# ConvFFN's two projections by Strassen's scheme, in two stages with the gated product in DRAM scratch

## The chip, the cores and the metric

The kernel runs on one core of a Trainium2 chip. The metric is device time in microseconds (us) of one execution; lower is better. The core's engines work side by side and wait for each other through semaphores: PE multiplies matrices into PSUM, DVE and POOL do elementwise work, ACT does elementwise functions, SP issues DMAs. DVE and ACT read PSUM; POOL works on SBUF alone.

## The reference, cut to what matters

One layer of a diffusion backbone with 1024 latent tokens of width 1024 and a 256-token context. The change concerns its last part:

```python
D_MODEL, SEQ, GRID_W, D_FF = 1024, 1024, 64, 2816

def conv_ffn(h, rows, w_up, conv_w, conv_b, w_down):
    b, n, _ = h.shape
    u = (h @ w_up).reshape(b, rows, n // rows, 2 * D_FF)      # 1024 -> 5632
    u = dwconv2d(u, conv_w, conv_b).reshape(b, n, 2 * D_FF)   # 3x3 depthwise, 16 x 64 grid
    gate, val = jnp.split(u, 2, axis=-1)
    return (jax.nn.gelu(gate) * val) @ w_down                 # 2816 -> 1024

...
x = x + g1 * merge_mixers(...)                                # ends in the output projection
x = x + g2 * conv_ffn(modulate(x, norm2_g, sh2, sc2), rows, ffn_w_up, ffn_conv_w, ffn_conv_b, ffn_w_down)
return rms_norm(x, final_g)
```

All of it is float32.

## The kernel before, in words

**Products.** Each float32 operand is split into two parts of type fp32r, hi + lo (`Weight.split`, `copy`, `sub`: ACT rounds to hi, DVE or POOL subtracts to get lo), and each block product is three matmuls, hi*hi + hi*lo + lo*hi (`mm3`). A matmul takes a 128x128 block of weights and 512 columns.

**Up-projection.** The 5632 channels are 44 tiles of 128: 22 pairs n of a gate tile and a value tile. A unit (`ffn_mm`) is one tile for all 1024 tokens: 8 blocks of the input width x 2 halves of the tokens x 3 = 48 matmuls into a PSUM tile `big` of two banks (three such tiles, and two of one bank, `sm`). Norm2's output stands transposed in SBUF (`H2`, written by `turn`), as hi and lo.

**Convolution.** `conv` starts each tile on ACT (the middle tap, with the bias), then eight taps follow on DVE, each one instruction that reads the unit in PSUM and adds to an accumulator in SBUF (L1391). `glu` applies gelu on ACT and multiplies gate by value on POOL (L1398; the last on DVE); the product is split into hi and lo and stays in SBUF (`G`).

**Down-projection.** For each two pairs, `down` multiplies 8 token tiles x 2 halves of the width x 2 blocks x 3 = 96 matmuls, and DVE adds each result to the residual `x[t]` in SBUF (L1475). `w_rows` multiplies the weights by the gate g2 on POOL (L97). So up- and down-products alternate, and a pair's taps lie between the down-products' adds. `down_last` takes the final norm along.

**Order.** Instructions are issued in the order of the code; each engine works through its own in order. SBUF is a set of slots of 4 KB per partition (`Slots`), handed out first in, first out. Weights are loaded and split ahead of use (`ahead`).

## Time and profile before

| | |
|---|---|
| time, median of 3 runs | 1547.22 us (1543.91 to 1547.32) |
| profiled execution, first to last instruction (its span) | 1541.3 us |
| what lies around the span: median less span | 5.9 us |
| PE busy | 1465.7 us, 95% |
| DVE busy | 1085.6 us, 70% |
| ACT busy | 523.7 us, 34% |
| POOL busy | 529.0 us, 34% |
| DMA | 109.30 MB, 71 GB/s over the span |

The profiled execution has no time of its own beside its span; the 5.9 us are taken for it. A busy share is an average over stages, so each stage has to be read by itself. ConvFFN's first convolution starts at 803 us, so the stage that changes is nearly half of the span.

### The profile page before, as it was taken

The page shows a single profiled execution, that of the slowest core. Times are in us where ns is not written, and L with a number is a line of the kernel's source. Part 1 is how long each engine was busy: PE and PEld are TensorE (multiplying, and loading weights), DVE is VectorE, ACT ScalarE, POOL GpSimd, SP SyncE. Part 2 cuts the span into 40 slices and gives each one's busy share as a digit, 9 for nine tenths or more (in the row PEclk, how much of TensorE's full clock was granted, in tenths as well). Part 3 has the DMA queues.
Part 4 walks back from the last instruction along what each step waited for, and adds up shares of the span by engine and source line. Part 5 has one row for each costly group of instructions (what it writes and reads, how often), then busy time and mean ns, then how long its engine had stood idle before and what let it go on. Part 6 is the DMA issues. An engine that isn't in the chain of part 4 may idle for free.

```text
span 1541.3 us, 16621 instructions
## 1 busy us (share of the span) xinstructions
PE 1465.7 (95%) x6725; PEld 1187.5 (77%) x6725; DVE 1085.6 (70%) x1193; ACT 523.7 (34%) x616; POOL 529.0 (34%) x269
## 2 busy tenths in 40 slices
PE   5999999998999689979999999999999999999994
PEld 4788888877888578868878787887878888887873
DVE  5768677856125986496668786868668686776887
ACT  6566777663110123242243130312222121222224
POOL 2211221122001553283053454425444342533343
PEclk9999999999999899999999999999999999999997
DMA  9211111101115344513030210112011111211102
GB/s 380 92 34 35 35 35 42 41 28 55 41 41 187 129 130 144 187 41 110 28 123 14 69 55 28 55 42 68 28 55 55 36 46 42 69 42 41 41 1 110
DMA packets 35069, 109.30 MB, mean 71 GB/s; under 512 B 3813, under 2 KB 8224, under 8 KB 34992
## 3 DMA queue, kind: packets, MB, share of 16 engines
q1 hardware_dynamic: 33552, 105.88, 20.2%
q10 hardware_dynamic: 1184, 2.11, 0.5%
q8 instruction: 53, 0.87, 0.2%
q0 software_dynamic: 256, 0.25, 0.1%
q14 instruction: 24, 0.20, 0.0%
HBM read 104.02 MB, written 4.19 MB: 70 GB/s over the span
## 4 chain that ended last, share of the span: by engine, by line
PE 53%; DVE 5%; ACT 1%; issue 1%; DVEq 0%; ACTq 0%
PE big L192 38%; PE sm L192 14%; DVE s L1234 1%; DVE t L453 1%; DVE s L136 1%; ACT s L1505 0%; PE sm L1318 0%; DVE s L336 0%; PE big L1221 0%; DVE s L1233 0%; DVE s L1232 0%; DVE s L1235 0%; DVE h2f L1323 0%; DVE s L1509 0%; DVE s L1311 0%
## 5 line engine op out<-in xcount | busy, mean ns | idle before, releaser
L192 PE MATMUL big<-s,s 128*128 128x512 f32 (+1 forms) x4548 | 1071.0, 395 | 9.8 <-DVE s L136 7.1
L192 PEld LDWEIGHTS big<-s,s 128*128 128x128 f32 (+1 forms) x4548 | 849.3, 188 | 211.2 <-DVE s L136 8.8
L1391 DVE SCALAR_TENSOR_TENSOR s<-big,rest,s 128x945 f32<-128x945 f32 (+2 forms) x352 | 429.2, 1220 | 120.4 <-issue 74.3
L136 POOL TENSOR_TENSOR s<-s,s 128x1024 fp32r<-128x1024 f32 (+1 forms) x132 | 316.9, 2418 | 294.4 <-ACT s L129 143.7
L129 ACT ACTIVATE s<-s 128x1024 fp32r<-128x1024 f32 (+4 forms) x170 | 167.5, 1022 | 261.9 <-DVE mid L921 62.1
L192 PE MATMUL sm<-s,s 128*128 128x512 f32 (+1 forms) x1176 | 253.4, 375 | 0.0
L192 PEld LDWEIGHTS sm<-s,s 128*128 128x128 f32 x1176 | 204.3, 188 | 47.6 <-DVE s L1475 6.2
L1378 ACT ACTIVATE s<-big,rest 128x1024 f32<-128x1024 f32 x44 | 53.1, 1207 | 428.2 <-PE big L192 428.2
L1398 POOL TENSOR_TENSOR s<-s,s 128x1024 f32<-128x1024 f32 x21 | 50.4, 2401 | 313.4 <-DVE s L1391 313.4
L1475 DVE TENSOR_TENSOR s<-sm,s 128x512 f32<-128x512 f32 x160 | 109.9, 687 | 53.7 <-PE sm L192 53.7
L136 DVE TENSOR_TENSOR s<-s,s 128x1024 fp32r<-128x1024 f32 (+3 forms) x62 | 92.0, 1492 | 65.3 <-ACT s L129 51.7
L791 POOL TENSOR_TENSOR s<-s,s 128x1280 f32<-128x1280 f32 x8 | 25.3, 3156 | 190.9 <-ACT s L787 190.9
L908 POOL TENSOR_TENSOR s<-s,s 128x1024 f32<-128x1024 f32 x8 | 21.1, 2644 | 127.4 <-PE big L192 120.7
L754 DVE SCALAR_TENSOR_TENSOR s<-big,par,s 128x1023 f32<-128x1023 f32 (+1 forms) x24 | 30.8, 1282 | 34.2 <-ACT s L751 33.6
L97 POOL TENSOR_TENSOR s<-s,s 128x1024 f32<-128x1024 f32 x22 | 53.1, 2412 | 0.0
L894 DVE TENSOR_TENSOR s<-big,s 128x1024 f32<-128x1024 f32 x8 | 9.8, 1224 | 61.1 <-PE big L192 61.1
L336 DVE SCALAR_TENSOR_TENSOR s<-s,s,s 128x1024 f32<-128x1024 f32 x28 | 43.5, 1555 | 1.0 <-DMA s<-in_mod_w_dram 0.5
L786 ACT ACTIVATE s<-big,rest 128x1024 f32<-128x1024 f32 x32 | 35.8, 1117 | 24.7 <-PE big L192 17.8
L816 DVE SCALAR_TENSOR_TENSOR s<-s,s 128x1280 f32<-128x1280 f32 x16 | 23.7, 1479 | 16.2 <-ACT s L812 16.2
L192 PE MATMUL big<-s,ghi 128*128 128x512 f32 x128 | 34.9, 394 | 0.0
L1221 PE MATMUL big<-s,s 126*128 126x512 f32 (+2 forms) x104 | 26.6, 353 | 8.3 <-DVE s L1233 8.3
L637 ACT ACTIVATE s<-big 128x1024 f32<-128x1024 f32 x8 | 8.1, 1022 | 67.6 <-PE big L192 60.8
(187 smaller groups left out, 1013.3 us busy)
## 6 DMA issues: line engine op xcount, KB each, us to landing
s<-in_mod_w_dram SPq DMA_DIRECT2D x48, 512.0 KB, 4.8
s<-in_ffn_w_up_b_dram SPq DMA_DIRECT2D x44, 512.0 KB, 3.5
s<-in_w_in_b_dram SPq DMA_DIRECT2D x32, 512.0 KB, 4.5
s<-in_ffn_w_down_dram SPq DMA_DIRECT2D x22, 512.0 KB, 3.4
s<-in_x_dram SPq DMA_DIRECT2D x16, 512.0 KB, 5.8
s<-in_w_lru_out_b_dram SPq DMA_DIRECT2D x8, 512.0 KB, 3.4
s<-in_w_o_dram SPq DMA_DIRECT2D x8, 512.0 KB, 5.8
out_dram<-s SPq DMA_DIRECT2D x5, 512.0 KB
```

The source lines that it names most:

```text
L97: self.k.nc.gpsimd.tensor_tensor(self.raw, self.raw, self.scale(), op=OP.mult)
L129: self.nc.scalar.activation(out, in_, AF.Copy)
L136: (self.nc.vector if eng == "dve" else self.nc.gpsimd).tensor_tensor(out, a, b, op=OP.subtract)
L192: return [lambda x=x: nc.tensor.matmul(x[0], x[1], x[2], start=x[3], stop=x[4]) for x in calls]
L336: nc.vector.scalar_tensor_tensor(self.acc, t, col, self.acc, op0=OP.mult, op1=OP.add)
L754: nc.vector.scalar_tensor_tensor(u[:, lo:hi], z[:, lo + s:hi + s], tap[t], u[:, lo:hi], op0=OP.mult, op1=OP.add)
L786: nc.scalar.activation(lat, ps, AF.Sigmoid, bias=col)
L1221: nc.tensor.matmul(x, w, y, start=id(x) not in seen, stop=id(x) not in [id(c[0]) for c in calls[i + 1:]])
L1378: nc.scalar.activation(acc, ps, AF.Identity, bias=self.par["fcb"][:, ti:ti + 1], scale=self.fcw(4, ti))
L1391: nc.vector.scalar_tensor_tensor(o, i, w, o, op0=OP.mult, op1=OP.add))
L1398: (nc.gpsimd if eng == "pool" else nc.vector).tensor_tensor(g, g, v, op=OP.mult)
L1475: nc.vector.tensor_tensor(x, ps, x, op=OP.add)
```

## The change

Strassen's scheme replaces the 8 block products of a 2x2 by 2x2 block product by 7, with sums of blocks ahead of and behind them.

- **Up.** The 2x2 blocks are: gate and value tile of pair n; halves of the input width; halves of the tokens. `turn0` and `turn1` form the token side once (B11, T1, T2, T3, B21, B22, T4, as hi and lo). Per pair, POOL forms the weights' sums (`up_sums`, and one in `up_split`), POOL makes all their lo parts, and `up_product` does 7 products of 4 x 3 = 12 matmuls of 512 columns. Partial sums are kept in PSUM; ACT copies four banks, DVE adds two (`up_join`). Each pair takes two of four PSUM tiles that fill PSUM.
- **The product goes to DRAM** (`G[n]`, stored by `glu`); the residual goes there too (`x1`) and is read again later. All of the up-stage comes before the down-stage.
- **Down.** Seven products one after the other, in the order 1, 2, 6, 7, 5, 4, 3 (`DOWN`), each a sum over 11 steps i (two blocks of `G`); a step is 4 x 3 = 12 matmuls. For each step `down_load` brings blocks of `G` (or the sums S2, S3 stored in DRAM scratch), `down_prep` forms sums on DVE and splits both operands: hi by ACT, lo of `fa` by POOL, lo of `fb` by DVE. `evacuate` combines the results of a product during the next one, with g2 applied by POOL, and does the final norm.

The core of the diff (names of the unchanged helpers as before):

```diff
+        def turn1(kp, pss):
...
+            v.tensor_tensor(f11, f12, f11, op=OP.subtract)
+            split("T1", kp, f11, "dve")
+            v.tensor_tensor(t2, f22, f11, op=OP.subtract)
+            split("T2", kp, t2, "dve")
+            v.tensor_tensor(f12, f22, f12, op=OP.subtract)
+            v.tensor_tensor(f21, f21, t2, op=OP.subtract)
+            split("T3", kp, f12, "pool")
+            split("B22", kp, f22, "pool")
+            split("T4", kp, f21, "dve")
...
+    PRODUCTS = (("A11", "B11", "a0"), ("S1", "T1", "v1"), ("S2", "T2", "a1"), ("A12", "B21", "a0"),
+                ("S3", "T3", "v0"), ("S4", "B22", "a1"), ("A22", "T4", "v0"))
...
+    def up_join(self, n):
+
+        nc, u = self.nc, self.U[n]
+        for b, x in (("a1", "p5"), ("v1", "u3")):
+            o = self.bank(n, b)
+            nc.vector.tensor_tensor(o, o, u[x], op=OP.add)
...
+                if n:
+                    if i == 1:
+                        self.taps(n - 1, "gt", 8)
...
+                    if i == 4:
+                        self.taps(n - 1, "vt", 5)
+            self.up_join(n)
+            if n:
+                self.taps(n - 1, "vt", 8)
+                self.gelu(n - 1)
+        self.down()
...
+    def down_ahead(self, s, loads=4, preps=2):
...
+        elif p == 2:
+
+            y = st[0]
+            v.tensor_tensor(x[:, 1], y[:, 0], y[:, 1], op=OP.subtract)
+            nc.sync.dma_start(self.S3[i], x[:, 1])
+            v.tensor_tensor(we[:, L], we[:, R], we[:, L], op=OP.subtract)
+            fb = wo[:, L]
+        elif p == 6:
+
+            v.tensor_tensor(fa, fa, x[:, 1], op=OP.subtract)
+            nc.sync.dma_start(self.S2[i], fa)
+            fb = x[:, 1]
+            v.tensor_tensor(fb, wo[:, R], we[:, L], op=OP.subtract)
...
+        for f, eng in ((fa, "pool"), (fb, "dve")):
+            t = sl.get([128, 2, 512], F32R, any_=True)
+            self.copy("act", t[:, 0], f)
+            self.sub(eng, t[:, 1], f, t[:, 0].bitcast(F32))
...
+        def add(t, d, bank, other):
+
+            e = H[d]
+            r = temp()
+            v.tensor_tensor(r, bank, other, op=OP.add)
+            nc.gpsimd.tensor_tensor(r, r, self.g2row[:, e], op=OP.mult)
+            v.tensor_tensor(y[t][:, e], y[t][:, e], r, op=OP.add)
+            square(t, d)
...
+                elif p == 4:
+                    add(4 + j, 0, b, at(w, j))
+
+                    r = temp()
+                    nc.gpsimd.tensor_tensor(r, at(u, j), self.g2row[:, H[1]], op=OP.mult)
+                    nc.gpsimd.tensor_tensor(y[j][:, H[1]], y[j][:, H[1]], r, op=OP.add)
...
+                self.down_ahead(s, *((4, 2) if p != 3 else (6, 5)))
...
+                mm(s, bank, range(4), i == 0, i == 10)
+                sl.free(*self.ready.pop(s))
+                s += 1
+                if i == 1 and before:
+                    evacuate(*before)
```

In the last product (p = 3) the last four steps are done together, token tile by token tile, so that `evacuate` of the first tile can start before the last is done.

The change moves instructions on each engine. Three places follow; names are tiles (`s_...` an SBUF slot, `ug` and `uv` a pair's PSUM tiles, `dn` a PSUM tile of the down-stage, `r` a temporary, `big` and `sm` the PSUM tiles of before).

DVE in the middle of ConvFFN, before: the taps of a pair (L1391) between the adds of the down-products (L1475).

```order
L1475 TENSOR_TENSOR s_5490<-sm,s_5490 128x512 x2
L1391 SCALAR_TENSOR_TENSOR s_8130<-big,rest,s_8130 128x15x63
L1391 SCALAR_TENSOR_TENSOR s_8394<-big,rest,s_8394 128x15x63
L1391 SCALAR_TENSOR_TENSOR s_8394<-big,rest,s_8394 128x960
L1391 SCALAR_TENSOR_TENSOR s_8394<-big,rest,s_8394 128x15x63
```

DVE at the end of a pair n of the up-stage now (L1532 is a tap, L1512 a join; `s_8262` is the value accumulator of pair n - 1, `s_8407` the gate accumulator of pair n):

```order
L1532 SCALAR_TENSOR_TENSOR s_8262<-uv,rest,s_8262 128x16x63 x2
L1512 TENSOR_TENSOR ug<-ug,p_8302 128x512
L1512 TENSOR_TENSOR uv<-uv,u_8361 128x512
L1532 SCALAR_TENSOR_TENSOR s_8262<-uv,rest,s_8262 128x15x63
L1532 SCALAR_TENSOR_TENSOR s_8262<-uv,rest,s_8262 128x960
L1532 SCALAR_TENSOR_TENSOR s_8262<-uv,rest,s_8262 128x15x63
L1532 SCALAR_TENSOR_TENSOR s_8407<-ug,rest,s_8407 128x15x63
```

The adds of the down-products have left this stretch; DVE goes from 16 taps of one pair through two joins to 16 taps of the next.

DVE in the seven forms of the tokens now, first of four blocks (L1353 to L1358 are the sums of `turn1`, L138 the lo parts; nothing of it stood before the change):

```order
L1353 TENSOR_TENSOR s_5317<-s_5668,s_5317 128x512
L138 TENSOR_TENSOR s_5650<-s_5317,s_5648 128x512
L1355 TENSOR_TENSOR t_5679<-s_5668,s_5317 128x512
L138 TENSOR_TENSOR s_5654<-t_5679,s_5652 128x512
L1357 TENSOR_TENSOR s_5668<-s_5668 128x512
L1358 TENSOR_TENSOR s_5317<-s_5317,t_5679 128x512
L138 TENSOR_TENSOR s_5666<-s_5317,s_5664 128x512
```

These seven come four times before the first pair's products can be finished.

DVE in the down-stage now, product 6, where the results of product 2 are taken (L1675 and L1678 form a step's sums, L138 is lo of `fb`, L1741 and L1743 are the two halves of `add`):

```order
L1675 TENSOR_TENSOR s_9553<-s_9553 128x512
L1678 TENSOR_TENSOR s_9553<-s_9254,s_8907 128x512
L138 TENSOR_TENSOR s_9600<-s_9553,s_9600 128x512
L1741 TENSOR_TENSOR r<-dn,s_9331 128x512
L1743 TENSOR_TENSOR s_9618<-s_9618,r 128x512
L1741 TENSOR_TENSOR r<-dn,s_9331 128x512
L1743 TENSOR_TENSOR s_9620<-s_9620,r 128x512
```

and POOL at the same place (L138 is lo of `fa`, L1742 the factor g2 of `add`):

```order
L138 TENSOR_TENSOR s_9547<-s_9505,s_9547 128x512
L138 TENSOR_TENSOR s_9573<-s_9529,s_9573 128x512
L138 TENSOR_TENSOR s_9597<-s_9553,s_9597 128x512
L1742 TENSOR_TENSOR r<-r,s_4445 128x512 x4
L138 TENSOR_TENSOR s_9653<-s_9579,s_9653 128x512
```

Before the change POOL had no part in adding results to the residual, and DVE made no sums of operands.

## Rows read from the trace of the kernel before

**Rows 1.** The page's first line.

```profile
span 1541.3 us, 16621 instructions
```

**Rows 2.** Windows: a stretch in the middle of ConvFFN, busy time by engine, clock, DMA.

```profile
core 0: us, PE busy (x) PEld busy (x) DVE busy (x) ACT busy (x) POOL busy (x), PEclk, DMA share, GB/s
1000.00:1200.00 200.00, 200.00 (x864) 160.96 (x863) 146.01 (x145) 43.59 (x42) 85.98 (x36) 1.00 0.15 48
```

**Rows 3.** Timeline, 1000 to 1070: start, length, engine, line, what, count, idle before.

```profile
1008.55 44.62 PE L192 MATMUL big<-s,s 128*128 128x512 f32 x192
...
1021.16 10.03 DVE L1391 SCALAR_TENSOR_TENSOR s<-big,rest,s 128x945 f32<-128x945 f32 x8 [10.61 <-issue]
...
1053.01 17.37 PE L192 MATMUL sm<-s,s 128*128 128x512 f32 x74
```

**Rows 4.** DVE reading PSUM: taps (ns min/median/max), adds (mean), and two in a row.

```profile
L1391 DVE SCALAR_TENSOR_TENSOR s<-big,rest,s x352: 1191/1206/1271, 804.1 to 1498.8; 128x945 f32<-128x945 f32 x88, 128x1008 f32<-128x1008 f32 x44, 128x960 f32<-128x960 f32 x44
...
L1475 DVE TENSOR_TENSOR s<-sm,s 128x512 f32<-128x512 f32 x160 | 109.9, 687 | 53.7 <-PE sm L192 53.7
...
1000.35 0.69 DVE L1475 TENSOR_TENSOR s<-sm,s 128x512 f32<-128x512 f32 x1 [0.31 <-PE sm L192]
1000.96 1.26 DVE L1391 SCALAR_TENSOR_TENSOR s<-big,rest,s 128x1008 f32<-128x1008 f32 x1
```

**Rows 5.** Timeline: DVE operations on SBUF beside POOL's, and one alone (748.81).

```profile
660.76 29.51 POOL L136 TENSOR_TENSOR s<-s,s 128x512 fp32r<-128x512 f32 x13 [3.09 <-ACT s L129]
...
663.19 2.20 DVE L1235 TENSOR_TENSOR s<-s,s 128x1024 f32<-128x1024 f32 x1
...
672.02 2.32 DVE L136 TENSOR_TENSOR s<-s,s 128x1024 fp32r<-128x1024 f32 x1
...
748.81 0.69 DVE L136 TENSOR_TENSOR s<-h2f,s 128x512 fp32r<-128x512 f32 x1
...
1510.03 2.40 POOL L1506 TENSOR_TENSOR s<-s,s 128x1024 f32<-128x1024 f32 x1 [26.99 <-ACT s L1505]
...
1510.42 2.03 DVE L453 TENSOR_TENSOR t<-r 128x1 f32<-128x1 f32 x1
```

**Rows 6.** Groups by form: an ACT copy, the convolution's start, a POOL subtraction (mean ns).

```profile
L129 ACT ACTIVATE s<-s 128x512 fp32r<-128x512 f32 x16 | 9.2, 624 | 27.7 <-DVE s L1235 23.6 <-issue 4.1
...
L1378 ACT ACTIVATE s<-big,rest 128x1024 f32<-128x1024 f32 x44 | 53.1, 1207 | 428.2 <-PE big L192 428.2
...
L136 POOL TENSOR_TENSOR s<-h2f,s 128x512 fp32r<-128x512 f32 x4 | 5.2, 1289 | 8.2 <-DVE h2f L1323 8.2
```

**Rows 7.** Timeline, from the output projection to ConvFFN's first convolution.

```profile
787.87 0.33 PE L1318 MATMUL sm<-ident,s 128*128 128x128 f32 x1 [1.61 <-DVE s L1311]
...
788.24 0.78 ACT L1322 ACTIVATE s<-sm,cols,a 128x512 fp32r<-128x512 f32 x1 [3.42 <-PE sm L1318]
...
802.89 1.21 ACT L1378 ACTIVATE s<-big,rest 128x1024 f32<-128x1024 f32 x1 [1.94 <-PE big L192]
```

**Rows 8.** Windows as in Rows 2: heavy loads at the start, and a wait of PE.

```profile
10.00:20.00 10.00, 6.62 (x36) 6.04 (x37) 5.64 (x18) 8.20 (x15) 0.00 (x0) 1.00 1.03 406
20.00:30.00 10.00, 6.93 (x61) 4.90 (x59) 7.86 (x14) 6.33 (x11) 3.27 (x2) 1.00 1.03 420
...
550.00:555.00 5.00, 2.72 (x14) 2.05 (x13) 3.28 (x5) 1.60 (x3) 2.57 (x2) 0.94 0.32 98
555.00:560.00 5.00, 5.00 (x30) 4.80 (x30) 4.90 (x9) 0.00 (x0) 0.76 (x2) 0.72 0.63 189
```

**Rows 9.** Timeline, the end: square sums, their root, the last scaling.

```profile
1531.28 0.58 ACT L1525 ACTIVATE sm<-s 128x512 f32<-128x512 f32 x1
1531.80 0.19 ACT L1525 ACTIVATION_READ_ACCUMULATOR sm<-s 128x1 f32 x1
1532.57 0.15 DVE L1536 TENSOR_TENSOR ss<-ss,half 128x1 f32<-128x1 f32 x1
...
1534.15 3.08 DVE L1509 SCALAR_TENSOR_TENSOR s<-s,r,s 128x512 f32<-128x512 f32 x3
```

More of the change, by code (lines that the diff above doesn't have):

```diff
@@ L1313, in turn, with rest, form @@
-        def turn(c, k):
-            if k % 2 == 0:
-                H2[c, k // 2] = [sl.get([128, 2, 512], F32R, any_=True) for _ in range(2)]
-            ps = self.sm()
+            def rest():
+                nc.vector.tensor_scalar(n, x[t], r(), None, op0=OP.mult)
+                nc.sync.dma_start(self.x1[t], x[t])
+                sl.free(x[t])
+            return rest
+        self.B = {}
+        f0 = {}
+        def form(name):
+            self.B[name] = [[sl.get([128, 2, 512], F32R, any_=True) for _ in range(2)] for _ in range(2)]
@@ L1352, in out_proj @@
                     ws[i // 6].done()
-                    if i < 24:
-                        self.ahead(4, 2, 2)
+                    if i // 6 < len(early):
+                        early[i // 6]()
             if t == 7:
@@ new lines, in out_proj @@
+        for n in range(2):
+            self.up_banks(n)
+        for n, bank in ((0, "a1"), (0, "v0"), (1, "a1")):
+            self.up_touch(n, bank)
+        for i in (0, 3):
+            self.up_product(0, i)
+        vt = self.U[1]["v"]
+        pss = [vt[:, 0:512], vt[:, 512:]]
+        for kp in range(4):
+            turn1(kp, pss)
+            if kp in (0, 2):
+                self.up_product(1, 0 if kp == 0 else 3)
+        self.up_touch(1, "v0")
+    PRODUCTS = (("A11", "B11", "a0"), ("S1", "T1", "v1"), ("S2", "T2", "a1"), ("A12", "B21", "a0"),
+                ("S3", "T3", "v0"), ("S4", "B22", "a1"), ("A22", "T4", "v0"))
@@ new lines, in up_banks, with bank, up_touch, up_product @@
+    def up_banks(self, n):
+        u = self.U[n]
+        u["g"], u["v"] = [self.pp.tile([128, 1024], F32, name=x, tag="up", bufs=4) for x in ("ug", "uv")]
+    def bank(self, n, b):
+        t = self.U[n]["g" if b[0] == "a" else "v"]
+        return t[:, 512:] if b[1] == "1" else t[:, 0:512]
+    def up_touch(self, n, b):
+        x = self.B["B11"][0][0][:, 0, :]
+        self.nc.tensor.matmul(self.bank(n, b), x[:, 0:128], x, start=True, stop=True)
+    def up_product(self, n, i):
+        nc, u = self.nc, self.U[n]
+        name, form, b = self.PRODUCTS[i]
+        w, (bh, bl) = u["w"].pop(name), self.B[form]
+        o = self.bank(n, b)
+        fresh = i in (0, 1)
+        for k in range(4):
+            hi, lo = [w[:, j, k * 128:(k + 1) * 128] for j in range(2)]
+            h, l = [x[k // 2][:, k % 2, :] for x in (bh, bl)]
+            for m, (x, y) in enumerate(((hi, h), (hi, l), (lo, h))):
+                first = fresh and k == 0 and m == 0
+                nc.tensor.matmul(o, x, y, start=first, stop=k == 3 and m == 2, skip_group_check=not fresh)
+        self.sl.free(w)
+        if i == 0:
+            self.copy("act", self.bank(n, "a1"), o)
+        elif i == 1:
+            u["p5"] = self.gp.tile([128, 512], F32, name="p5", tag=("ghi", "graw")[n % 2])
+            self.copy("act", u["p5"], o)
+        elif i == 2:
+            self.copy("act", self.bank(n, "v0"), o)
+        elif i == 4:
+            u["u3"] = self.gp.tile([128, 512], F32, name="u3", tag=("glo", "rb")[n % 2])
+            self.copy("act", u["u3"], o)
@@ new lines, in gelu, with glu, taps @@
+    def gelu(self, n):
+        g = self.U[n]["ga"]
+        self.nc.scalar.activation(g, g, AF.Gelu_apprx_tanh)
+    def glu(self, n):
+        nc, u = self.nc, self.U[n]
+        nc.gpsimd.tensor_tensor(u["ga"], u["ga"], u["va"], op=OP.mult)
+        self.sl.free(u["va"])
+        nc.sync.dma_start(self.G[n], u["ga"])
+        self.sl.free(u["ga"])
+        del self.U[n]
+    def taps(self, n, x, count):
+        t = self.U[n][x]
+        for _ in range(min(count, len(t))):
+            t.popleft()()
@@ new lines, with down_plan @@
+    DOWN = (1, 2, 6, 7, 5, 4, 3)
+    def down_plan(self):
+        self.st = {}
+        self.wd = {}
+        self.S2 = [self.dp.tile([128, 512], F32, name=f"S2_{i}") for i in range(11)]
+        self.S3 = [self.dp.tile([128, 512], F32, name=f"S3_{i}") for i in range(11)]
+        self.dl = self.dq = 0
+        self.steps = [(p, i) for p in self.DOWN for i in range(11)]
+        self.ready = {}
+    def down_ahead(self, s, loads=4, preps=2):
+        n = len(self.steps)
+        while True:
+            if self.dq < self.dl and self.dq < min(n, s + preps + 1) and self.sl.room_all() >= 2:
+                self.down_prep(self.dq)
+                self.dq += 1
+            elif self.dl < min(n, s + loads + 1) and self.sl.room_all() >= 5:
+                self.down_load(self.dl)
+                self.dl += 1
+            else:
+                break
```

502 lines of the change are left out of this document (291 added, 211 removed).

## The prediction

> **What bounds the kernel now.** I read first the windows over ConvFFN: in 200 us PE is busy for all 200, DVE for 146, POOL for 86, ACT for 44, at a granted clock of 1.00 (the upper level, 2.4 GHz) [rows 2]. So matmuls set the time of this stage. Their price comes from the timeline: 192 matmuls take the time from 1008.55 to 1053.01, 0.2316 us each [rows 3]. ConvFFN has 2112 matmuls up and 1056 down; at this price 734 us of the span of 1541.3 [rows 1]. The second thing to see is DVE: 146 of 200 us is little slack. Its taps cost 10.03 us for eight, 1.254 us each [rows 3], and hardly vary (1.19 to 1.27 us) whatever POOL does [rows 4].
>
> The third is how DVE and POOL go together. In the merge before the output projection POOL needs 29.51 us for 13 subtractions of 512 columns, 2.27 us each [rows 5], where one alone takes 1.29 [rows 6]; DVE's operations of 1024 columns on two SBUF tiles take 2.2 to 2.3 us beside it, and one of 512 alone 0.69 (so about 1.25 for 1024). Thirteen times 1.28 plus ten times 1.25 is 29.2: the two engines take turns, an operation at a time. The end shows it as clearly: a DVE operation on a single column, L453, lasts 2.03 us, until POOL's of 1510.03 ends at 1512.43 [rows 5]. The taps and the adds read one tile in PSUM and one in SBUF and are not held up [rows 4]. So for this kernel: **DVE operations with both inputs in SBUF, and POOL's, add up; those with an input in PSUM don't.**
>
> **The change, part by part.**
>
> *Matmuls.* Up 22 x 7 x 12 = 1848 (and four to open banks), down 7 x 11 x 12 = 924: 396 fewer, 91.7 us if PE stays the bound. A pair up is 84 matmuls, 19.45 us; a step down is 12, 2.78 us.
>
> *Up to the first pair.* The norm of the last tokens ends at 787.87, as before [rows 7]. Then `turn1` forms its operands for four blocks. DVE can begin at 790.0: 8 transposes and two ACT operations of 0.78 us [rows 7] lie ahead. I take 0.62 us for a DVE operation of 512 columns behind another (the next starts 0.61 later [rows 4]), 0.69 where another engine waits for it, 0.62 for an ACT copy and 1.28 for POOL's [rows 6], and 0.05 for each hand-over. A block: sum, ACT copy, lo part, 0.69 + 0.05 + 0.62 + 0.05 + 0.62 = 2.03 us, for T1 and again for T2; then a sum (0.62), and POOL's subtraction waits for the ACT copy until 0.67 behind it; POOL, DVE's last lo part and POOL again take turns, 0.67 + 1.28 + 0.62 + 1.28 = 3.85. Together 8.5 us; four blocks 34, to 824.0. PE has 48 matmuls of this time and mostly waits. POOL then has two lo parts of the first pair's weights (826.6), and PE the products S3 and S4: the first needs those lo parts from 825.3 on and ends at 827.6, the second at 830.4. Before, the first convolution began at 802.9 [rows 7]; now DVE's join (0.69) and ACT's start (1.21 [rows 6]) put the first tap at 832.4. **So 28 us are lost here**, nothing hides them, since no other products are there.
>
> *The pairs.* DVE has 16 taps and two joins a pair, 16 x 1.254 + 2 x 0.62 = 21.3 us; PE has 19.45. Before, the down-products' matmuls lay beside the taps; now none do. The next pair needs the PSUM tiles of the last but one, so PE can lead no further: its second product waits for the last three taps. From there it needs five products, 13.9 us, until the join can run, and DVE has 13 taps, 16.3 us, in front of it; so DVE never waits, and is the bound. 336 taps and 42 joins: 421.3 + 26.0 = 447.3 us. **The up-stage ends at 1279.7**, 1.9 us a pair above PE's. POOL has 11 operations of 512 and one of 1024 a pair, some 16.5 us, beside taps that it doesn't hold up; ACT about 11.
>
> *The down-stage, from DVE and POOL.* PE's part is 77 x 2.78 = 214 us, 30.6 a product. A step costs:
> - Products 2, 6, 5, 3: `fa` is a sum, so the chain is DVE's sum 0.69, ACT 0.62, POOL's lo 1.28 and DVE's lo behind it 0.62, with hand-overs 3.3 us. A second sum of DVE fits into ACT's time.
> - Product 4: two sums, 0.62 + 0.69, POOL 1.28, lo 0.62: 3.2. Product 7: one sum, 2.6, so PE's 2.78. Product 1 has no sums.
>
> Steps are prepared two ahead, so a delay of some 3 us is covered, not one that repeats. What DVE needs, counted from 1279.7:
> - Product 1: the last pair's 16 taps (20.1) and eight lo parts with about 0.3 of waiting each (7.4): 27.5.
> - Product 2: a step loads 1.31 MB and stores 0.26 MB. DMA reached 406 to 420 GB/s at most [rows 8]; at 410 that is 3.84 us a step. Two steps are loaded early: 2 x 3.3 + 9 x 3.84 = 41.2, to 68.7.
> - Product 6: 36.4, and `evacuate` of product 2: four times DVE's add, POOL's g2, DVE's add, 0.69 + 1.28 + 0.69 + 0.1 = 2.75, during which DVE's queue stands: 11.0. To 116.1.
> - Product 7: 31.1, its four adds from PSUM within; to 147.2. Product 5: 36.4 + 2.5 = 38.9, to 186.1.
> - Product 4: 35.2 + 4 x 3.33 (one more add) = 48.5, to 234.6.
> - Product 3: 36.4, and between its steps `evacuate` of product 4, four times three POOL operations and a DVE one, 4 x 4.46 = 17.8, and the norm of four token tiles, 1.7 + 4 x 1.25 = 6.7; to 295.5. The loads of its last three steps stand on SP behind the stores of these tiles, so they cannot come earlier.
> - The end: 12 matmuls (2.8), then four token tiles one after the other on DVE and ACT, each 0.69 + 0.69 + 0.58 + 0.19 for the sum of squares, 1.58 to the root (1532.57 to 1534.15 [rows 9]), 1.25 for scaling and 0.3 of hand-overs, 5.3: 21.2; and the last store, 4.1 as now (from 1537.23 to the span's end [rows 1, 9]). To 323.6.
>
> **Sum:** 1279.7 + 323.6 = 1603.3 us of span, 62 above 1541.3. The median lies 5.9 above the span, so 1609 us, 4.0% slower. The 92 us saved on PE are spent where PE waits: 28 at the entry, 41 in the pairs (21.3 against 19.45, 22 times), the rest, some 85, in the down-stage.
>
> On product 2 a page may be set against the rows. The rows reach 420 GB/s with a DMA share above 1.0 [rows 8]. The Trainium skill (DMA: Bandwidth & Descriptors, Specifications) gives some 358 GB/s per core as the limit of HBM. By it a step would be an estimated 4.4 us, product 2 five us longer and the time 1614. The rows decide, since this core has shown more.
>
> **Bounds of the unknown costs.** What no row shows is how well DVE, ACT and POOL pack such chains, and how far DVE gets ahead between products. Lower bound: only the turns count (1.28 per POOL operation, 0.62 per DVE one), with PE's 30.6 as the least. Products 2, 6 and 4 have 34.5, 42 and 42, 7 and 5 have 30.6, 3 has 51; with product 1 and the end 290 instead of 323.6: 1576. Upper bound: POOL gets in twice before a DVE operation, as the 2.3 us against 1.25 [rows 5] show once each time; one more 0.7 us on half of the 77 steps is 27, so 1636.
>
> **Rivals.**
> - *The taking of turns doesn't bind* (the other side): the operations of 512 columns interleave beside PE's steps and two steps of lead are enough. Then the down-stage is PE's 214 and 17 for the end (the first tiles are done while PE finishes): 1279.7 + 231 + 5.9 = 1517, 2% faster. For it: ACT and DMA have room. Against it: the rows at 660 and 1510, and the sums of product 2, 6 and 4, which exceed 30.6 with perfect packing. It decides at one point: the change gains if the down-stage, its end included, takes less than 261.6 us (1541.3 - 1279.7).
> - *Turns bind, but pack well*: the lower bound, 1560 to 1585.
> - *The clock falls.* PE will wait in each product. In the rows 2.3 us of waiting in 5 us was followed by 5 us at 0.72 [rows 8], some 1.4 us lost; at the level of 1.2 GHz a step takes 5.56 us instead of 2.78, more than DVE's 3.3, and PE would be the bound again. All 77 steps at that level: 428 us, 1738; after ten long waits only: 14 us, 1623. Against it: in both stretches at the start PE waited too, 3.4 and 3.1 us of 10, and the clock stayed at 1.00 [rows 8]. The Trainium skill (TensorE: Matmul & The Clock Gate, HAM oscillation) has the rule: idle stretches between groups of matmuls throttle the array again, each round. By that rule the down-stage's groups would start slow, and the time lies above 1640.
> - That fewer matmuls are issued is sure from the order of PE's instructions; that isn't a rival.
>
> **How the numbers follow.** A measurement of this kernel tells about 0.3% from no change. Chances: the chain as summed (1585 to 1640) 0.58; packing well 0.18; the clock or other waits, above 1640, 0.10; PE's bound, below 1543, 0.09; between 1543 and 1560 0.05, of which 0.03 within 0.3%. So faster 0.09, same 0.03, slower 0.88. The range 1555 to 1645 takes in both bounds, and leaves out the PE-bound case and most of the clock's.
>
> **What would show it.** The first tap near 832. In the up-stage DVE busy throughout, PE waiting some 2 us a pair, pairs 21.3 us apart. In the down-stage DVE subtractions and sums of 1.3 to 2 us instead of 0.69, POOL waiting in turn, PE idle a third of the time with long waits in products 6, 4 and 3; DMA near 400 GB/s in product 2. The forecast is wrong if pairs come 19.5 us apart, if these DVE operations last 0.69 beside POOL's, or if the down-stage with its end takes under 262 us.

## The result, and the profile after

1664.3 us (median of four runs, 1658.6 to 1666.4) against 1546.2: the ratio is 1.0762, 95% interval 1.0741 to 1.0784. **7.6% slower**, where 4.0% had been forecast, and above the range. The profiled run took 1658.6 us with a span of 1656.6, so 2.0 us lie around the span and not the 5.9 that the forecast added: in the later runs of the kernel before, time and span lie 1.7 to 1.8 us apart too, and its profiled execution was a shorter one than the median. The page of the changed kernel, the first lines (busy time, share of the span, instructions):

```profile
span 1656.6 us, 17205 instructions
...
PE 1431.0 (86%) x6333; PEld 1128.0 (68%) x6333; DVE 1210.6 (73%) x1298; ACT 665.3 (40%) x953; POOL 704.8 (43%) x497
```

PE fell from 95% to 86%. In the middle of the up-stage, the stretch of [rows 2], the windows now show DVE at 182 of 200 us, and PE no longer full:

```profile
1000.00:1200.00 200.00, 179.37 (x751) 140.35 (x749) 182.06 (x160) 82.42 (x124) 145.75 (x107) 0.99 0.20 71
```

DVE is not full either. The timeline of DVE, and of PE, over one pair shows what both wait for (start, length, ..., idle time before):

```profile
1060.67 0.69 DVE L1512 TENSOR_TENSOR ug<-ug,p 128x512 f32<-128x512 f32 x1
1062.76 0.70 DVE L1512 TENSOR_TENSOR uv<-uv,u 128x512 f32<-128x512 f32 x1 [1.40 <-PE uv L1494]
1063.36 3.68 DVE L1532 SCALAR_TENSOR_TENSOR s<-uv,rest,s 128x945 f32<-128x945 f32 x3
1066.96 10.02 DVE L1532 SCALAR_TENSOR_TENSOR s<-ug,rest,s 128x945 f32<-128x945 f32 x8
1076.90 6.29 DVE L1532 SCALAR_TENSOR_TENSOR s<-uv,rest,s 128x945 f32<-128x945 f32 x5
1083.10 0.69 DVE L1512 TENSOR_TENSOR ug<-ug,p 128x512 f32<-128x512 f32 x1
...
1059.72 2.93 PE L1494 MATMUL uv<-s,s 128*128 128x512 f32 x12
1062.49 2.94 PE L1494 MATMUL ug<-s,s 128*128 128x512 f32 x12
1067.19 3.01 PE L1494 MATMUL uv<-s,s 128*128 128x512 f32 x12 [1.77 <-DVE s L1532]
```

The join of the value tile adds to bank v1. It waits 1.40 us until PE's product of 1059.72 is done, which is the seventh and writes bank v0 of the same tile. The three value taps of the pair before, which wait for nothing, stand behind the join; PE in turn waits 1.77 us for them. A pair takes 22.43 us (1060.67 to 1083.10).

In the down-stage the first DVE operation of each product, in the order 2, 6, 7, 5, 4, 3 (ns min/median/max, first and last start), gives the time of each:

```profile
L1669 DVE TENSOR_TENSOR s<-s x11: 677/692/693, 1344.4 to 1384.8; 128x512 f32<-128x512 f32 x11
L1675 DVE TENSOR_TENSOR s<-s x11: 676/678/682, 1388.0 to 1433.0; 128x512 f32<-128x512 f32 x11
L1682 DVE TENSOR_TENSOR s<-s,s x11: 684/1774/1801, 1436.3 to 1469.6; 128x512 f32<-128x512 f32 x11
L1685 DVE TENSOR_TENSOR s<-s x11: 673/678/685, 1472.8 to 1507.7; 128x512 f32<-128x512 f32 x11
L1690 DVE TENSOR_TENSOR s<-s,s x11: 684/1766/1795, 1511.0 to 1562.1; 128x512 f32<-128x512 f32 x11
L1694 DVE TENSOR_TENSOR s<-s x11: 676/678/693, 1565.9 to 1623.8; 128x512 f32<-128x512 f32 x11
```

L1682 and L1690 have a median of 1.77 us where the others have 0.68. The timeline shows the reason in product 7: the sum starts just behind POOL's and is done when POOL has finished and 0.5 us more have passed.

```profile
1439.46 1.28 POOL L138 TENSOR_TENSOR s<-s,s 128x512 fp32r<-128x512 f32 x1 [1.95 <-ACT s L131]
1439.50 1.79 DVE L1682 TENSOR_TENSOR s<-s,s 128x512 f32<-128x512 f32 x1
...
1442.69 1.30 POOL L138 TENSOR_TENSOR s<-s,s 128x512 fp32r<-128x512 f32 x1 [1.95 <-ACT s L131]
1442.73 1.80 DVE L1682 TENSOR_TENSOR s<-s,s 128x512 f32<-128x512 f32 x1
```

### The profile page after: what moved, and what is told of

Same layout as the page of the kernel before. It is cut to its first block, busy times and chain, and to the rows that moved or that the text cites. A ratio compares the mean times of both kernels' runs of the same rounds, so it can differ in the third digit from the quotient of the medians.

```text
span 1656.6 us, 17205 instructions
## 1 busy us (share of the span) xinstructions
PE 1431.0 (86%) x6333; PEld 1128.0 (68%) x6333; DVE 1210.6 (73%) x1298; ACT 665.3 (40%) x953; POOL 704.8 (43%) x497
## 5 line engine op out<-in xcount | busy, mean ns | idle before, releaser
L138 POOL TENSOR_TENSOR s<-s,s 128x512 fp32r<-128x512 f32 (+1 forms) x284 | 422.8, 1498 | 482.7 <-ACT s L131 405.1
L194 PE MATMUL big<-s,s 128*128 128x512 f32 (+2 forms) x2352 | 558.3, 395 | 10.2 <-DVE s L138 5.6
L194 PEld LDWEIGHTS big<-s,s 128*128 128x128 f32 (+2 forms) x2352 | 437.6, 189 | 116.0 <-DVE s L138 7.0
L131 ACT ACTIVATE s<-s 128x512 fp32r<-128x512 f32 (+2 forms) x406 | 265.2, 697 | 351.2 <-DVE mid L907 62.8
L1800 PE MATMUL dn<-s,s 128*128 128x512 f32 x924 | 247.4, 418 | 81.6 <-ACT s L131 56.1
L138 DVE TENSOR_TENSOR s<-s,s 128x512 fp32r<-128x512 f32 (+2 forms) x154 | 186.7, 1217 | 140.6 <-ACT s L131 113.7
L1494 PE MATMUL ug<-s,s 128*128 128x512 f32 x1056 | 264.0, 399 | 15.1 <-ACT uv L131 14.4
L1494 PEld LDWEIGHTS ug<-s,s 128*128 128x128 f32 x1056 | 199.2, 190 | 69.0 <-ACT uv L131 23.0
L1494 PE MATMUL uv<-s,s 128*128 128x512 f32 x792 | 200.7, 403 | 39.9 <-DVE s L1532 37.7
L1532 DVE SCALAR_TENSOR_TENSOR s<-ug,rest,s 128x945 f32<-128x945 f32 (+2 forms) x176 | 214.9, 1221 | 5.3
L1532 DVE SCALAR_TENSOR_TENSOR s<-uv,rest,s 128x945 f32<-128x945 f32 (+2 forms) x176 | 214.7, 1220 | 4.6
L131 ACT ACTIVATE u<-uv 128x512 f32<-128x512 f32 x22 | 13.2, 600 | 102.8 <-PE uv L1494 102.8
```

The lines of the kernel that those rows point to most:

```text
L131: self.nc.scalar.activation(out, in_, AF.Copy)
L138: (self.nc.vector if eng == "dve" else self.nc.gpsimd).tensor_tensor(out, a, b, op=OP.subtract)
L194: return [lambda x=x: nc.tensor.matmul(x[0], x[1], x[2], start=x[3], stop=x[4]) for x in calls]
L1494: nc.tensor.matmul(o, x, y, start=first, stop=k == 3 and m == 2, skip_group_check=not fresh)
L1532: nc.vector.scalar_tensor_tensor(o, i, w, o, op0=OP.mult, op1=OP.add))
L1800: nc.tensor.matmul(bank(j), x, z, start=first and m == 0, stop=end and m == 2)
```

## The experiments

Each is an edit of the changed kernel or of an earlier edit, beside which its time is put. The four runs of the changed kernel lie 8 us apart, so a single run decides nothing smaller.

**e1: the late join** (0 is the gate tile's join and `conv`, 1 the value tile's)

```diff
...
-            self.up_join(n)
+            self.up_join(n, 0)
             if n:
                 self.taps(n - 1, "vt", 8)
                 self.gelu(n - 1)
+            self.up_join(n, 1)
```

> The join of the value tile (and the start of its convolution) moves behind the last three value taps of the pair before, so that DVE has work while PE does the seventh product. Theory (DVE sets the pair, and stands still for about 1.4 us in each because the join waits for the seventh product in the other half of the same PSUM tile): gate joins 21.3 us apart instead of 22.65, the wait of L1512 for uv gone, PE's wait per pair up to 1.8 us unchanged or smaller; 21 x 1.3 = 27 us less, 1637 us. Rival (PE sets the pair, and DVE's wait costs nothing): the joins stay 22.6 apart and the time stays within 5 us of 1664.

Measured: 1632.7 us (ratio to the kernel before 1.0569, 1.0552 to 1.0587), 31.6 less than 1664.3. The wait is gone and the joins come 20.93 us apart. DVE's queue, idle nowhere in this stretch:

```profile
1065.66 0.69 DVE L1512 TENSOR_TENSOR ug<-ug,p 128x512 f32<-128x512 f32 x1
1066.25 3.68 DVE L1534 SCALAR_TENSOR_TENSOR s<-uv,rest,s 128x945 f32<-128x945 f32 x3
1069.85 0.69 DVE L1512 TENSOR_TENSOR uv<-uv,u 128x512 f32<-128x512 f32 x1
1070.45 10.02 DVE L1534 SCALAR_TENSOR_TENSOR s<-ug,rest,s 128x945 f32<-128x945 f32 x8
...
1086.59 0.69 DVE L1512 TENSOR_TENSOR ug<-ug,p 128x512 f32<-128x512 f32 x1
```

**e2: one tap of eight less** (a single run)

```diff
-                if dy == 0 and dx == 0:
+                if dy == 0 and dx == 0 or dy == 1 and dx == 1:
                     continue
```

> As e1, and one of the eight taps of each tile is left out (that for the lower right neighbour), which takes 2 x 1.25 us from DVE per pair and nothing from PE. Theory (DVE is the bound): the pair falls from 21.3 to PE's own 84 x 0.2316 = 19.5 us or slightly above, 19.7, so 33 us less than e1, and 2.5 us less in the first product of the down-stage: about 1600 us. Rival (PE, by its waits on ACT and POOL or by its clock, sets the pair): no difference from e1.

Measured: 1617.8 us, 15 less than e1, neither 33 nor 0. The windows of e1, then of e2, over the same 200 us:

```profile
950.00:1150.00 200.00, 190.30 (x804) 149.13 (x803) 195.63 (x172) 87.57 (x133) 157.50 (x116) 1.00 0.21 75
```

```profile
950.00:1150.00 200.00, 193.42 (x827) 154.34 (x826) 176.72 (x157) 91.03 (x136) 162.31 (x119) 1.00 0.22 79
```

So in e1 DVE is the bound, at 196 of 200, and in e2 PE is: pairs come 20.4 us apart, and from the fourth pair on the gate tile's join waits for PE in each, 1.9 us in most. PE's own pair is not 19.5, for it waits some 0.75 us in each for ACT's copy from bank to bank (15.3 us in 20 pairs). DVE's 20.93 stands barely above it.

**e3: one matmul of three in the down-stage** (a single run)

```diff
-                for m, (x, z) in enumerate(((hi, fb[:, 0]), (hi, fb[:, 1]), (lo, fb[:, 0]))):
-                    nc.tensor.matmul(bank(j), x, z, start=first and m == 0, stop=end and m == 2)
+                nc.tensor.matmul(bank(j), hi, fb[:, 0], start=first, stop=end)
```

> In the down-stage the matmuls hi*lo and lo*hi are left out: 308 matmuls for 924; all copies, sums, low parts and loads stay. Theory (the chain DVE, ACT, POOL sets the down-stage, and DMA in product 2): steps of products 6, 7, 5 and 4 stay at 3.2 to 3.9 us; only the last 48 matmuls (16 now) and the little that PE has to catch up behind each combination go: 10 to 20 us less, 1645 to 1655. Rival (PE at the clock it is granted sets the down-stage): 616 x 0.2316 = 143 us less, about 1520; at half the clock for the matmuls that are left, still about 1590.

Measured: 1654.8 us, 10 less than the median of the changed kernel and 4 less than its lowest run. Two thirds of the stage's matmuls cost next to nothing. The windows from 1350 to 1550, first of the changed kernel, then of e3:

```profile
1350.00:1550.00 200.00, 157.96 (x595) 112.61 (x594) 135.00 (x154) 65.52 (x119) 76.29 (x57) 0.91 0.55 198
```

```profile
1350.00:1550.00 200.00, 99.57 (x192) 55.80 (x192) 135.35 (x155) 64.62 (x118) 75.56 (x57) 0.50 0.54 197
```

In e3 the granted clock is at its lower level (1.2 GHz, 0.50) throughout, and PE is still idle half of the time. PE's busy time, with all that the lower clock adds to it, falls by 58 us in these 200, and the time hardly moves: neither PE nor its clock sets this stage in the changed kernel.

**e4: the low part of `fa` on DVE**

```diff
-        for f, eng in ((fa, "pool"), (fb, "dve")):
+        for f, eng in ((fa, "pool" if p == 1 else "dve"), (fb, "dve")):
```

> In products 2, 6, 7, 5, 4 and 3 of the down-stage the low part of fa is made by DVE instead of POOL. Theory (DVE's sums and POOL's low parts take turns, a difference of 512 columns costing 1.3 to 1.5 us on POOL and 0.69 on DVE alone): a step with two sums goes from 3.24 and 3.9 us to about 3.0 (four operations of 0.69 and a wait for ACT's copy), one with a single sum to PE's 2.78; 2 + 5 + 5 + 8 + 3 us less in products 6, 7, 5, 4, 3, and some of the combinations: about 25 us less, 1640. Rival (DVE's throughput is the bound and nothing is shared): DVE has one operation more per step, 66 x 0.69 = 45 us more, 1700 or, where PE hides half of it, 1685.

Measured: 1620.4 us (1.0485, 1.0470 to 1.0501), 43.9 less, more than expected, though DVE has 66 operations more. From the groups of 1400 to 1550 us, first of the changed kernel, then of e4:

```profile
L138 POOL TENSOR_TENSOR s<-s,s 128x512 fp32r<-128x512 f32 x37 | 50.7, 1372 | 72.9 <-ACT s L131 64.5 <-issue 4.6 <-DMA s<-G 3.7
...
L138 DVE TENSOR_TENSOR s<-s,s 128x512 fp32r<-128x512 f32 x37 | 36.5, 987 | 35.2 <-ACT s L131 29.6 <-issue 5.6
L1682 DVE TENSOR_TENSOR s<-s,s 128x512 f32<-128x512 f32 x11 | 18.5, 1681 | 0.0
```

```profile
L138 DVE TENSOR_TENSOR s<-s,s 128x512 fp32r<-128x512 f32 x93 | 62.6, 690 | 16.1 <-ACT s L131 14.6
...
L1682 DVE TENSOR_TENSOR s<-s,s 128x512 f32<-128x512 f32 x11 | 7.5, 684 | 0.0
```

DVE's operations last 0.69 us as soon as POOL has nothing beside them, and one of DVE's takes the place of one of 1.37 on POOL. Counted as above, product 7 takes 24.9 us (1434.7 to 1459.6) for 36.5, product 4 takes 43.7 (1491.2 to 1534.9) for 54.9. The edit removes the turns and the slower engine in the chain together and does not tell their shares apart: product 5, whose sum lasts 0.68 in both, falls from 38.2 to 31.6 too.

**e5: e1 and e4 together**

> The edits of e1 and e4 together: the late join of the value tile, and the low part of fa on DVE in the down-stage. Theory (two separate losses, one in each stage): the savings add up, 31 from the one and 44 from the other: 1664 - 75 = 1589 us. Rival (both remove the same wait, or an earlier start of the down-stage runs into loads that come later): clearly less than the sum, 1600 to 1615.

Measured: 1595.1 us (1.0313, 1.0296 to 1.0330), 69.2 less than 1664.3; the sum would be 75.5. Most of the two savings adds up: they are separate losses.

**e6: all first additions ahead in the combinations of products 2 and 5** (`rest` is called for the four token tiles at the end of `evacuate`; a single run)

```diff
...
-            v.tensor_tensor(y[t][:, e], y[t][:, e], r, op=OP.add)
-            square(t, d)
+            def rest():
+                v.tensor_tensor(y[t][:, e], y[t][:, e], r, op=OP.add)
+                square(t, d)
+            return rest
...
```

> In the combinations behind products 2 and 5, all four first additions are issued before the first of the additions that wait for POOL's g2, so that DVE's queue does not stand in each of the four. Theory (DVE, in its order, sets the down-stage, so what its queue stands is lost): 12.7 and 13.2 us fall to about 7 (POOL's four of 1.27 us and one addition each side), PE's waits at the product behind them fall by as much, about 12 us less: 1652. Rival (PE has work enough in hand, or the loads behind set the pace): no change, 1664.

Measured: 1651.5 us, 7 below the lowest run of the changed kernel. Behind product 2 the combination takes 7.95 us for 12.7, and PE's longest wait up to 1550 us falls from 12.4 to 7.6. Of the 12.7 us, 3.29 are a wait for the load of the residual, which the prediction's 11.0 did not have:

```profile
1404.85 0.69 DVE L1743 TENSOR_TENSOR s<-s,r 128x512 f32<-128x512 f32 x1 [3.29 <-DMA s<-x]
```

With all first additions ahead of it, 1.06 us of this wait are left.

**e7: no POOL work for the first pairs' weights** (in `up_sums`, then in `up_split`; a single run)

```diff
+        if n < 2:
+            u["x"] = self.sl.get([128, 1024], any_=True)
+            return
...
-        self.sub("pool", w[:, 1], src, w[:, 0].bitcast(F32))
+        if not (n == 0 and i < 4 or n == 1 and i in (0, 3)):
+            self.sub("pool", w[:, 1], src, w[:, 0].bitcast(F32))
...
```

> For the first two pairs POOL's sums of weights, and the low parts of the six that are formed before the up-stage, are left out (the raw block and the high part are used in their place). Theory (these take turns with the DVE operations of the last norm of the output projection, whose inputs lie in SBUF too, which made its last scaling end at 792.9 instead of 787.9): the first tap moves from 840.4 to about 835, 5 us less at the end: 1659. Rival (the output projection's own end or its loads set the start): first tap and time unchanged.

Measured: 1659.3 us; first tap 838.1 for 840.4. The last norm does end at 787.88, but PE then has two products of pair 0 ahead of the first transposes, and the first block starts only 2.3 us sooner. Whether those count in the end a single run can't tell.

**e8: product 2 without the even block of `G`** (a single run)

```diff
-            nc.sync.dma_start(t.rearrange("p a b -> p (a b)"), G[0])
...
-            v.tensor_tensor(x[:, 1], y[:, 0], y[:, 1], op=OP.subtract)
+            v.tensor_tensor(x[:, 1], x[:, 0], wo[:, R], op=OP.subtract)
```

> In product 2 the load of the even block of G (512 KB of 1.5 MB per step) is left out; the difference that goes to S3 is formed of other data. Theory (DMA sets product 2: 3.9 us a step, 1.5 MB at about 410 GB/s): steps fall to what two sums and the low parts take, 3.24 us as in product 6, 11 x 0.7 = 8 us less: 1656. Rival (DVE and POOL set product 2 as they do product 6, its DMA waits being slack): within 3 us of 1664.

Measured: 1650.3 us, 8 below the lowest run of the changed kernel; the steps of product 2 take 3.42 us (L1668, 1342.5 to 1376.7) for 4.04 (L1669 above). DMA did bind product 2, and what binds behind it lies close.

**e9 and e10**, each on e5: S3 formed by POOL behind the gated product; the norm of token tiles 4 to 7 behind the last preparations

```diff
...
         nc.gpsimd.tensor_tensor(u["ga"], u["ga"], u["va"], op=OP.mult)
+        if n % 2 == 0:
+            d = u["va"][:, 0:512]
+            nc.gpsimd.tensor_tensor(d, u["ga"][:, 0:512], u["ga"][:, 512:1024], op=OP.subtract)
+            nc.sync.dma_start(self.S3[n // 2], d)
...
```

(The lines of e9 that are not shown take the load of the even block, the difference and its store out of product 2.)

```diff
                 sl.free(*w)
-                norm(4, 4)
...
                         self.dq += 1
+                    norm(4, 4)
                     for j in range(4):
```

> On top of both edits (late join, low part of fa on DVE; 1595 us): the difference S3 of two halves of an even block of G is formed in the up-stage by POOL, right behind the gated product, and stored from there, so that product 2 neither loads the even block (512 KB of 1.5 MB a step) nor forms the difference. Theory (DMA sets product 2, 4.3 us a step in that run): its steps fall to PE's 2.78, about 10 to 13 us less, 1584. Rival (POOL's extra 1.4 us per two pairs delays the gated products, or PE has so much to catch up that nothing is gained): 1593 or more.

> On top of both edits (1595 us): the final norm of token tiles 4 to 7, with its four stores, moves from behind the combination of product 4 to behind the preparations of the last four steps. Theory (PE waits 19.5 us ahead of the last 48 matmuls because these preparations stand in DVE's order behind the combination and the norm, 6.5 us, and their loads on SP behind the stores): the wait falls by 6 us, the norm hides behind the 48 matmuls: 1589. Rival (the wait is due to the loads of product 3 or to the combination alone): 1595.

Measured: e9 1574.0 us (1.0187, 1.0165 to 1.0209), 21 less than e5, where some 10 to 13 had been expected; the steps of product 2 fall from 4.3 us to 2.1 on DVE (L1673, 1319.1 to 1339.9), less than PE's 2.78, so DVE gets ahead: PE's longest wait between 1320 and 1420 us falls from 12.1 us in e5 to 3.3. How much of the 21 is the load, and how much DVE's operation and the store, e9 does not tell. e10 1587.8 us (1.0277, 1.0256 to 1.0298), 7 less; PE's wait ahead of the last 48 matmuls falls from 19.5 to 13.2 us.

**e11: e5, e6, e9 and e10 together**

> All at once: late join, low part of fa on DVE, combinations of products 2 and 5 with their first additions ahead, S3 formed in the up-stage, late norm. Theory (separate losses, each on the path): 1595 - 11 - 8 - 6 = 1570 us, still slower than before by 1.5%. Rival (with one wait gone the next takes its place, PE being busy nine tenths of the down-stage by then): 1580 or more.

Measured: 1557.9 us (1.0083, 1.0064 to 1.0102). The losses add up, about: 37 below e5, where the parts gave 7 (one run), 21 and 7.

**e12 and e13**, on e11: PE adds the second product to the gate tile; then also ACT's start of that convolution behind the sixth product, and DVE's join kept for pair 0

```diff
...
+            q = u["p5s"] = self.sl.get([128, 2, 512], F32R, any_=True)
+            self.copy("act", q[:, 0], u["p5"])
+            self.sub("pool", q[:, 1], u["p5"], q[:, 0].bitcast(F32))
+        elif i == 5:
+            q = u.pop("p5s")
+            for m in range(2):
+                nc.tensor.matmul(o, self.idr, q[:, m], start=False, stop=m == 1, skip_group_check=True)
...
```

```diff
...
                 self.up_product(n, i)
+                if i == 5:
+                    self.up_join(n, 0)
...
```

> As e11, and the addition of the second product to the gate tile is done by PE, with two matmuls by the identity of its high and low part (ACT copies it once more, POOL forms the low part), instead of by DVE's join. Theory (DVE sets the pair, 21.3 us; PE needs 19.5 and two matmuls of 0.23, and waits 0.76 for ACT's copies): the pair falls by DVE's 0.65 to 20.7, where PE's own 20.7 meets it: 21 x 0.65 = 13 us less, 1557. Rival (PE's 86 matmuls, its wait for ACT or POOL at nine tenths busy set the pair): no gain or a loss, 1570 to 1580. Faster than before (1546) by neither.

> As e12, with two things moved: ACT starts the gate tile's convolution right behind the sixth product of the pair (ahead of its copies for the next pair's weights), and the first pair keeps DVE's join. Theory (e12 won nothing because DVE, freed of its join, waited 0.71 us a pair for this start, which stood in ACT's order behind copies into slots that a store to DRAM still held, and because the first pair's two matmuls by the identity waited for ACT and POOL, some 6 us): DVE's pair falls from 21.3 to 20.7, first tap back at 840: 13 + 5 us less, 1540, which would be just faster than before (1545). Rival (PE's own 86 matmuls and its waits for ACT's copies already take 21.3): at most 5 us less, 1553.

Measured: e12 1557.9 us, e13 1555.7 us (1.0074, 1.0061 to 1.0087): no difference that can be told from e11. That e12 meets the 1557 expected for it is chance: 13 us were to come off 1570, and e11 had come in at 1557.9. In e12 DVE waits 0.4 to 1.0 us for ACT's start of the convolution, in every second pair and not in each, and the first pair's value join comes at 845.2 us for 839.6 in e11. Both are gone in e13. There the value join waits 0.2 to 0.3 us for PE in nearly every pair, and the pair takes 20.8 us, with PE busy for 193.3 and DVE for 193.0 of 200. The rival of e13 holds: PE's 86 matmuls and its waits for ACT set the pair there, a quarter of a microsecond above DVE's own work.

**e14: on e13, POOL's work for pair 1 moved behind the second block of `turn1`**, and pair 0's first two products behind the first

```diff
...
-                 lambda: self.up_sums(1), lambda: [self.up_split(1, q) for q in (0, 3)]]
...
+            if kp == 1:
+                self.up_sums(1)
+                for q in (0, 3):
+                    self.up_split(1, q)
...
```

> As e13, and POOL's sums and low parts for pair 1 move from the end of the output projection to behind the second block of the last transposition, and the first pair's first two products behind its first block. Theory (with POOL's work beside it the last norm ends 5 us late, and PE's two products stand ahead of the first transposes): the last norm ends near 788, the first block starts near 790 instead of 794, and what starts earlier stays earlier: 3 to 4 us less than e13. Rival (POOL's work, moved between the low parts of T3 and B22, holds up these, and the up-stage's start with them): no gain, or some us more.

Measured: 1561.8 us (1.0108, 1.0093 to 1.0123), 6 more. The first block starts at 791.3, for 794.5 in e13, but the second at 805.2 for 804.4, behind PE's two products, which now stand between the two. In the third block POOL's work stands beside DVE's, whose operations of 0.69 last up to 1.79, and the fourth starts at 827.1 for 820.9.

**e15 and e16**: on e11, the first three preparations of the down-stage behind the last pair's taps; then also the combination of product 4 ordered as in e6. **e17**: e16 with the edits of e13

```diff
-                    self.down_ahead(0)
+                    self.down_ahead(0, preps=2 if i > 4 else -1)
```

```diff
...
-                    add(4 + j, 0, b, at(w, j))()
+                    later.append(add(4 + j, 0, b, at(w, j)))
...
```

> As e11, and in the last pair the first three preparations of the down-stage come behind the sixth product instead of ahead of the last taps. Theory (in e11 the pairs are 20.93 us apart but the last one takes 29.8, because the low parts of these preparations stand in DVE's order ahead of 16 taps, wait for ACT's copies, and these for loads; DVE stands 8 us there): the last pair falls to about 21, 8 to 9 us less than e11's 1558: 1549. Rival (the last pair is long because of its loads and of PE's wait for slots, or the waits come back in the first product): at most 3 us less.

> As e15, and the combination behind product 4 is ordered like the other two: first the four first additions, then the four that wait for POOL's g2, POOL's eight other operations last. Theory (PE's wait of 13.6 us ahead of the last 48 matmuls comes from DVE's queue, which stands 16.5 us in this combination): DVE's stand falls to 7 or 8 us, PE's wait to about 5, 8 us less than e15: 1541, just faster than before (1545). Rival (POOL's 12 operations of 1.28 us, which then take turns with the sums and low parts of product 3, cost DVE as much as the order saves): as e15.

> As e16, on e13 instead of e11 (PE adds the second product to the gate tile, and ACT starts the convolution earlier). In e13 the pairs were 20.8 us apart for 20.93 in e11, and PE was busy for 96.65 us in 100. Theory by now (with DVE and PE at the same level, it's PE's 86 matmuls and its 0.7 us wait for ACT's copy that set the pair): 20 x 0.13 = 2 to 3 us less than e16. Rival (DVE still sets it): 13 us less.

Measured: e15 1551.7 us (1.0046, 1.0032 to 1.0059), 6 less than e11, for 8 to 9 expected: the last pair falls from 29.8 to 23.5 us. e16 1548.8 us (1.0032, 1.0021 to 1.0043), 3 less again, for 8 expected; the runs of the two overlap (1549.6 to 1554.3 and 1547.5 to 1553.1), but PE's wait ahead of the last 48 matmuls does fall, from 13.6 to 6.7 us. e17 1553.7 us (1.0053, 1.0041 to 1.0066), 5 more than e16, where its theory had 2 to 3 us less and its rival 13 less. Its pairs are 20.8 us apart as in e13, but its last pair takes 28.6 us between value joins for e16's 23.5, since DVE waits 3.5 us there for ACT's copies in the first preparations, and in the profiled run the first tap comes 3 us later. The best version, e16, has come back 115 us and still does not beat the kernel before, which stays 0.3% ahead.

## Why the prediction was right and wrong

The direction was right and, in the main, the cause: DVE's work in the pairs, and its turns with POOL, rather than PE's matmuls (e2, e3, e4). 53 us of span were missed, in three places. (The terms of the lower bound add up to 286 us and not 290, so 1572; nothing hangs on it.)

- **The entry, first tap 840.4 for 832.4.** The four blocks of `turn1` took 8.2 to 9.9 us for the 8.5 of the sum. Half of the 8.0 us is their start, 794.1 for 790.0. The row it was counted from, the norm's end at 787.87, does not hold: POOL's first work on weights takes turns with that norm, which ends at 792.85 (e7: 787.88). By e7 this is 2.3 us of the 4.1; the rest are PE's two products ahead of the transposes. The blocks add 0.7 us, PE's products behind them 1.6 (the sixth ends at 836.9, 8.0 behind the last block, for 6.4), and 1.5 the first pair's value join, which waits 2.1 us and stands ahead of the first tap.
- **"So DVE never waits, and is the bound": this step failed, and cost most.** The prediction let the join run five products after PE goes on, when its own bank is ready. The wait is for the whole tile: the value join stands until the seventh product of the pair, the sixth from there, has written the other bank, and PE waits 0.7 us more for ACT's copy on the way. That is 1.40 us a pair. Pairs took 22.43 us for 21.3, and 20.93 without the wait (e1, 31.6 us less). The last pair took 27.9 us, because the first preparations of the down-stage stand in DVE's order ahead of its taps; moving them gave 6 us (e15). In all the up-stage ended at 1317.6, and of the 38 us that it was late 30 lie here.
- **The down-stage: 339.0 us for 323.6**, from 1317.6:

| | product 1 | 2 | 6 | 7 | 5 | 4 | 3 | end |
|---|---|---|---|---|---|---|---|---|
| predicted | 27.5 | 41.2 | 47.4 | 31.1 | 38.9 | 48.5 | 60.9 | 28.1 |
| measured | 26.8 | 43.6 | 48.3 | 36.5 | 38.2 | 54.9 | 61.2 | 29.5 |

Six of eight terms were within 2.4 us. Products 7 and 4 were mis-sized by 12 us together. There the sum counted DVE's sums as 0.62 or 0.69; POOL's low part of the step before gets in first, and they take 1.77 (in e4, without POOL's part, 0.68). The upper bound allowed for this ("POOL gets in twice") in half of the 77 steps; it came in products 7 and 4, 22 of them.

- **DMA in product 2** went nearly as the rows said, 4.04 us a step for 3.84. From 1360 to 1380 us the windows of the changed kernel give 411 GB/s at a DMA share of 1.03:

```profile
1360.00:1380.00 20.00, 16.44 (x60) 11.77 (x58) 12.93 (x15) 5.90 (x11) 6.45 (x5) 0.91 1.03 411
```

The Trainium skill's 358 GB/s (DMA: Bandwidth & Descriptors, Specifications), there worked out as a stack's 716 GB/s divided by two cores, is not borne out as a limit for this core, which works alone. e8 shows the load on the path.

- **The rivals.** "Turns don't bind" fell with e4, and "pack well" with the table. "The clock falls" was partly there: the profiled run's windows of 50 us show 0.83 to 1.00 between 800 and 1600 us. In the down-stage e3 shows that it was not what set the time: with 58 us of PE's busy time gone in 200, what the clock adds included, at most 10 us came back. In the up-stage, at 0.93 to 1.00 from 850 us on, it was not tested apart. The time lies above 1640, where the prediction had "the clock or other waits" at 0.10; it was other waits, the 1.40 us a pair above all (e1).
- **What the 92 us of PE went into.** After the avoidable waits are removed (e16), the entry is still there (first tap 840.9 for 804.1 [rows 4]: 37 us, in part filled with products), the pairs take 20.93 for PE's 19.45 (22 times 1.5: 33 us), and at the end the last product must be combined and normed. The windows of e16 show where PE then stands:

```profile
800.00:840.00 40.00, 24.57 (x93) 18.99 (x94) 18.29 (x25) 22.16 (x37) 21.29 (x16) 0.79 0.17 53
840.00:1260.00 420.00, 397.44 (x1672) 311.80 (x1672) 410.50 (x362) 188.30 (x281) 339.68 (x251) 1.00 0.22 78
...
1300.00:1500.00 200.00, 190.07 (x807) 153.05 (x805) 178.77 (x257) 88.55 (x161) 27.31 (x19) 0.98 0.60 208
1500.00:1546.20 46.20, 17.63 (x48) 11.02 (x48) 33.29 (x63) 9.40 (x23) 10.63 (x7) 0.61 0.23 91
```

That is 15 us at the entry, 23 in the pairs, 10 in most of the down-stage and 29 at the end, with the clock below its upper level at the entry and the end; before, PE stood for none of 697 us from 803 to 1500, and for 20 of the last 41. That uses up the gain. This last account is worked out, not tested apart.

## What to carry to other kernels

When a change takes work from the full engine, count first what the next engine needs per unit: DVE's 20.93 us a pair left 1.5 of the 2.8 us that a pair saves on PE unusable before any wait. A wait was for a whole PSUM tile here, so put behind a join whatever does not need it, and look in each queue for ready work that stands behind a waiting instruction; e1, e6, e10, e15 and e16 only changed such orders and gave some 50 us. Work with two SBUF inputs given to POOL to relieve DVE was no relief where the two take turns: giving it back to DVE saved 44 us, the slower engine's part included.
